# Channel mixers of an encoder trunk: down of 28 of 32 hidden blocks in pairs, seven block products in place of eight

## The chip, the cores and the metric

One core of a Trainium2 chip runs the whole trunk. The metric is the device time of one execution in microseconds (us); the median of the runs counts.

## The reference

Two requests, 256 prompt tokens and 1024 sample tokens of 1024 channels in float32, pass two layers. Layer 0 mixes tokens by a bidirectional recurrent mixer (RWKV-7), layer 1 by neighbourhood attention; each is followed by the same kind of channel mixer, which is all that changes here:

```python
def _sq_relu_mlp(h, w_up, w_down):
    return jnp.square(jax.nn.relu(h @ w_up)) @ w_down
...
D_FF = 4 * D_MODEL
...
        x = x + y
        x = x + _sq_relu_mlp(_rms_norm(x, p['norm_mlp_g'][layer]), p['w_up'][layer], p['w_down'][layer])
```

## The kernel before

Activations lie transposed, channels on the 128 partitions and tokens along the free axis: 256 prompt tokens (segment 0) and two segments of 512 sample tokens (1 and 2). Float32 products are made of three matmuls in the float32r format: each operand is cut into a high part (a cast by ACT) and a low part (the difference, by DVE or POOL), and `mm3` (lines 95 to 97) adds high x high, high x low and low x high into one bank of PSUM. So every weight that is loaded is cut too (`wsplit`, lines 88 to 90: transfer, cast, low part).

`channel_layer` does, for each layer, the output projection of the token mixer, the channel mixer and the first work of what follows. The 4096 hidden channels go in 32 blocks of 128 (`f`). For a block, `up(f, s)` multiplies the up weights with the 8 x 128 input channels of a segment (`dense`, 24 matmuls), takes relu on ACT (line 1360), squares on POOL (1361) and cuts the result into `hh` and `hl` (1363 on ACT, 1364 on DVE). `down` multiplies the block's 128 hidden channels into 8 groups of 128 output channels (3 matmuls each) and DVE adds each group from PSUM to the running sum `x` (1382). The up weights of a block (512 KB) and its down weights (512 KB) are transferred once, on SP's queue, as one tile each.

`x` is kept divided by the norm's factor during the loop (`scale`, line 1347), and the factor is multiplied back at the end of the last `down` (1384). PSUM has eight banks: seven rotate for all products, one serves the norms. The loop from block 2 on runs up of block `f` and down of block `f - 1` for each segment; the last two blocks' downs are added in one bank. Instructions are put in order on each engine by a planner, by the order of the text and by when their operands will be there; only in the last part of each layer PE's order is that of the text:

```python
            for f in range(2, NF - 1):
                for s in range(3):
                    up(f, s)
                    down([f - 1], s)
                if rest and f > 4:
                    inverse(*rest.pop())
                wdown(f)
...
            with tc.manual_schedule(engines={mybir.EngineType.PE}):
```

A tile of a pool is one of `bufs` slots that share a `tag`; a tile that takes a slot waits until the slot's last users are done.

Of the kernel before, what the change touches and what calls it, by code (L numbers as in the profile page):

```python
# [13 lines left out]
P = 128  # L14
# [21 lines left out]

class Pieces:
# [11 lines left out]
class Trunk:  # L49
    def __init__(self, ctx, tc, a):  # L50
# [16 lines left out]
        self.dall = self.cp.tile([P, 8, 2, 20], F32, name="dall")  # L67
        self.bonus = self.cp.tile([P, 20, 8], F32, name="bonus")
# [436 lines left out]
    def v_block(self, act, vw, dst, tp, pp, q, tb, scale=1.0, later=False):  # L505

        nc = self.nc
        ps = pp[0].tile([P, 512], F32, name="vps", tag=pp[1])
# [648 lines left out]
    def add_squares(self, wk, x, m, s, acc, nsq=2):  # L1157
# [6 lines left out]
        else:  # L1164
            sq = wk.tile([P, 512], F32, name="sq", tag="sq", bufs=nsq)
# [11 lines left out]
    def token_norms(self, wk, wh_, pn, acc, s):  # L1177
# [8 lines left out]
        for j in range(2):  # L1186
            for b in range(nb):
                if j and b % 2 == 0:

                    w = 4 // nb  # L1190
                    pq = wh_.tile([P, 256], F32, name="pq", tag="hhFalse", bufs=2)
# [12 lines left out]
    def gate_begin(self):  # L1204
# [36 lines left out]
        def weight(m):  # L1241
            self.wo.append(self.wsplit(self.clw, self.a["w_o"][m], 1024, nc.gpsimd, tag="u"))
# [11 lines left out]
    def gated(self, wk, pm, src):  # L1254

        nc, act = self.nc, self.act
        with self.gctx, self.tc.tile_pool(name="go", bufs=1, reuse_waits="tile", side="right") as gp:
            (sh, sl, ss), (gh, gl, gs) = self.gate
            todo = [(0, k) for k in range(KT)] + [(s, k) for s in (1, 2) for k in range(KT - 1)] + [(1, KT - 1), (2, KT - 1)]
            for s, k in todo:  # L1260
# [5 lines left out]
                ps = pm.tile([P, 512], F32, name="ps", tag="ps")  # L1266
# [7 lines left out]
    def channel_layer(self, layer, x_src, src, wname, dst, gnext=None, gate=False):  # L1274
# [6 lines left out]
        with ExitStack() as ctx:  # L1281
# [7 lines left out]
            pn = ctx.enter_context(tc.tile_pool(name="cln", bufs=1, space=PSUM, reuse_waits="tile"))  # L1289
            wo = self.wo  # L1290
            if gate:
                self.gated(wk, pm, src)
# [13 lines left out]
            def dense(hi, lo, s):  # L1306
                c0, c1 = SEGS[s]
                n = c1 - c0
                ps = pm.tile([P, 512], F32, name="ps", tag="ps")
# [7 lines left out]
            for seg in ((0, 1), (2,)):  # L1317
                for m in range(8):
                    hi, lo = wo.pop(0)
                    if len(wo) < 1 and todo:  # L1320
                        wo.append(self.wsplit(wp, a[wname][todo.pop(0)], 1024, nc.vector, tag="u"))
# [9 lines left out]
                    for s in seg:  # L1331
# [3 lines left out]
                        self.add_squares(wk, x, m, s, ms[s], 2 + layer)  # L1335
# [17 lines left out]
            def up(f, s):  # L1353
                c0, c1 = SEGS[s]
                n = c1 - c0
                if s == 0:
                    wu[f] = self.wsplit(wp, a["w_up"][layer, f], 1024, nc.gpsimd, tag="u")
                ps = dense(*wu[f], s)
                r = wk.tile([P, 512], F32, name="rl", tag="nt", bufs=3 + layer)
                nc.scalar.activation(r[:, :n], ps[:, :n], AF.Relu)  # L1360
                nc.gpsimd.tensor_tensor(out=r[:, :n], in0=r[:, :n], in1=r[:, :n], op=ALU.mult)  # L1361
                hh, hl = (wh_.tile([P, c1 - c0], F32R, name=t, tag=f"{t}{s > 0}", bufs=4 if s else 2) for t in ("hh", "hl"))
# [558 lines left out]
```

## Time and profile before

| What | Value |
|---|---|
| median of 3 runs | 4051.72 us (4046.44 to 4057.34) |
| span of the profiled execution | 4029.3 us |
| median less span | 22.4 us |
| PE busy | 3805.9 us (94%) |
| DVE, ACT, POOL busy | 2244.2, 1580.9, 1338.7 us |
| MLP loop of layer 0 | about 1500 to 2400 us of the span |
| MLP loop of layer 1 | about 3140 to 4029 us of the span |

The profiled execution's own time is not listed beside its span; times are reckoned from the span and set beside the median of the runs. A row of a group gives the line, the engine, the operation, output and inputs, shapes and count, then busy time in us and mean duration in ns, then the engine's idle time before these instructions and what ended it. A row of a timeline gives start, duration, engine, line, operation; in brackets stands the idle time before it and what ended that. A row of windows gives for each engine its busy time in a stretch and, in parentheses, its instructions, then the clock granted to PE.

### The profile page before, as it was taken

What the parts mean: (1) busy time and instruction counts of PE and PEld (TensorE: products, weight loads), DVE (VectorE), ACT (ScalarE), POOL (GpSimd) and SP (SyncE); (2) the same over time, 40 slices, a digit from 0 to 9 for tenths busy, and PEclk for the clock granted to TensorE, in tenths of its full rate; (3) what the DMA queues carried; (4) which work ended last, traced back from release to release, by engine and by line L of the source; (5) the groups of instructions that cost most, each with busy time, mean ns of one, the idle gap of its engine ahead of it and who ended that gap; (6) DMA issues with size and microseconds to landing.
All of it is one profiled execution on the core that took longest, in us unless ns stands there. A gap on an engine that the chain in (4) does not pass through costs nothing.

```text
span 4029.3 us, 90997 instructions
## 1 busy us (share of the span) xinstructions
PE 3805.9 (94%) x36820; PEld 3210.5 (80%) x36820; DVE 2244.2 (56%) x4581; ACT 1580.9 (39%) x3868; POOL 1338.7 (33%) x1252
## 2 busy tenths in 40 slices
PE   8988898888888899999999999999989999999999
PEld 5764578778888788888888889887778888888888
DVE  5778743656564456555555561455554755555555
ACT  6776642555555431111111142565654111111111
POOL 4446542122222433222222250344443422222222
PEclk9987989999999999999999999999999999999999
DMA  4236565766664421101111015354463010110101
GB/s 140 72 104 221 207 222 137 171 171 160 161 153 118 146 79 37 42 32 42 37 37 43 32 71 165 103 124 98 101 199 129 35 42 35 39 42 32 42 32 63
DMA packets 450885, 394.89 MB, mean 98 GB/s; under 512 B 267456, under 2 KB 352832, under 8 KB 450464
## 3 DMA queue, kind: packets, MB, share of 16 engines
q1 hardware_dynamic: 416048, 327.72, 28.7%
q10 hardware_dynamic: 34416, 61.35, 4.1%
q8 instruction: 289, 4.73, 0.5%
q14 instruction: 132, 1.08, 0.1%
HBM read 270.50 MB, written 124.44 MB: 98 GB/s over the span
## 4 chain that ended last, share of the span: by engine, by line
PE 79%; DVE 6%; ACT 5%; DMA 4%; issue 4%; POOL 2%; SPq 1%; ACTq 0%; DVEq 0%; POOLq 0%
PE ps L95 19%; PE ps L96 19%; PE ps L97 19%; PE wu L997 4%; PE vps L512 1%; PE vps L513 1%; PE vps L514 1%; PE aps L997 1%; PE op L1836 1%; PE kps L997 1%; PE lps L997 1%; PE pt L1779 1%; PE ltw L598 1%; PE yps L997 1%; PE yo L997 1%
## 5 line engine op out<-in xcount | busy, mean ns | idle before, releaser
L1382 DVE TENSOR_TENSOR x<-ps,x 128x256 f32<-128x256 f32 x1488 | 814.5, 597 | 643.8 <-PE ps L97 643.7
L95 PE MATMUL ps<-ah,whi 128*128 128x512 f32 (+1 forms) x2304 | 843.2, 366 | 0.0
L96 PE MATMUL ps<-al,whi 128*128 128x512 f32 (+1 forms) x2304 | 825.5, 358 | 0.0
L97 PE MATMUL ps<-ah,wlo 128*128 128x512 f32 (+1 forms) x2304 | 822.6, 357 | 1.5 <-DVE wlo L90 1.3
L90 POOL TENSOR_TENSOR wlo<-raw,whi 128x1024 fp32r<-128x1024 f32 (+1 forms) x178 | 390.2, 2192 | 856.0 <-ACT whi L89 823.8
L95 PE MATMUL ps<-hh,whi 128*128 128x512 f32 (+1 forms) x1536 | 546.5, 356 | 9.8 <-DVE x L1382 9.8
L96 PE MATMUL ps<-hl,whi 128*128 128x512 f32 (+1 forms) x1536 | 545.6, 355 | 0.0
L97 PE MATMUL ps<-hh,wlo 128*128 128x512 f32 (+1 forms) x1536 | 545.1, 355 | 0.0
L95 PEld LDWEIGHTS ps<-ah,whi 128*128 128x128 f32 x2304 | 434.3, 188 | 72.4 <-issue 8.2
L97 PEld LDWEIGHTS ps<-ah,wlo 128*128 128x128 f32 x2304 | 433.4, 188 | 72.6 <-DVE wlo L90 1.7
L96 PEld LDWEIGHTS ps<-al,whi 128*128 128x128 f32 x2304 | 434.4, 189 | 62.3 <-issue 1.0
L89 ACT CAST whi<-raw 128x1024 fp32r<-128x1024 f32 (+1 forms) x206 | 200.4, 973 | 706.3 <-PE ps L96 627.7
L1361 POOL TENSOR_TENSOR rl<-rl 128x512 f32<-128x512 f32 (+1 forms) x192 | 173.8, 905 | 506.1 <-PE ps L97 462.4
L95 PEld LDWEIGHTS ps<-hh,whi 128*128 128x128 f32 x1536 | 290.7, 189 | 54.2 <-DVE x L1382 12.0
L97 PEld LDWEIGHTS ps<-hh,wlo 128*128 128x128 f32 x1536 | 291.0, 189 | 41.6
L96 PEld LDWEIGHTS ps<-hl,whi 128*128 128x128 f32 x1536 | 290.6, 189 | 40.5
L1360 ACT ACTIVATE rl<-ps 128x512 f32<-128x512 f32 (+1 forms) x192 | 100.7, 524 | 555.9 <-PE ps L97 555.9
L1363 ACT CAST hh<-rl 128x512 fp32r<-128x512 f32 (+1 forms) x192 | 105.6, 550 | 324.2 <-POOL rl L1361 324.2
L1364 DVE TENSOR_TENSOR hl<-rl,hh 128x512 fp32r<-128x512 f32 (+1 forms) x192 | 119.8, 624 | 143.1 <-ACT hh L1363 142.5
L1773 POOL TENSOR_TENSOR s<-s,mx 128x384 f32<-128x384 f32 (+1 forms) x150 | 109.7, 744 | 163.2 <-DVE mx L1772 114.2
L872 DVE TENSOR_TENSOR tmp<-mt,q 128x31 f32<-128x31 f32 (+15 forms) x310 | 117.2, 378 | 38.9 <-ACT mt L861 21.0
L1078 POOL TENSOR_TENSOR y<-y,mu 128x512 f32<-128x512 f32 x18 | 19.3, 1074 | 351.2 <-DVE mu L1075 351.2
(304 smaller groups left out, 8265.1 us busy)
## 6 DMA issues: line engine op xcount, KB each, us to landing
raw<-in_w_down_dram SPq DMA_DIRECT2D x64, 512.0 KB
raw<-in_w_up_dram SPq DMA_DIRECT2D x64, 512.0 KB
ar<-ar_d SPq DMA_DIRECT2D x80, 256.0 KB
bk<-bk_d SPq DMA_DIRECT2D x80, 256.0 KB
ar_d<-ar ACTq DMA_DIRECT2D x32, 512.0 KB
bk_d<-bk ACTq DMA_DIRECT2D x32, 512.0 KB
bs<-tab SPq DMA_DIRECT2D x128, 96.0 KB
v_d<-vt ACTq DMA_DIRECT2D x80, 128.0 KB
```

The lines of the kernel that those rows point to most:

```text
L89: nc.scalar.copy(hi[:, cs], raw)
L90: lo_eng.tensor_tensor(out=lo[:, cs], in0=raw, in1=hi[:, cs].bitcast(F32), op=ALU.subtract)
L95: mm(ps, sh, mh, start=first, stop=False)
L96: mm(ps, sh, ml, start=False, stop=False)
L97: mm(ps, sl, mh, start=False, stop=last)
L872: nc.vector.tensor_tensor(out=tv, in0=mt[:, 0:jj, jj:jj + 1].to_broadcast([P, jj, w]), in1=q[:, jj:jj + 1, jj:].to_broadcast([P, jj, w]), ...
L997: self.nc.tensor.matmul(out, w, x, start=start, stop=stop, skip_group_check=free)
L1361: nc.gpsimd.tensor_tensor(out=r[:, :n], in0=r[:, :n], in1=r[:, :n], op=ALU.mult)
L1363: nc.scalar.copy(hh[:, :n], r[:, :n])
L1364: nc.vector.tensor_tensor(out=hl[:, :n], in0=r[:, :n], in1=hh[:, :n].bitcast(F32), op=ALU.subtract)
L1382: nc.vector.tensor_tensor(out=xv, in0=ps[:, :n], in1=xv, op=ALU.add)
L1773: nc.gpsimd.tensor_tensor(out=s[:, :nk], in0=s[:, :nk], in1=mx[:, 2:3].to_broadcast([P, nk]), op=ALU.mult)
```

## The change

For blocks 2 to 29, two blocks are taken as a pair. Their down on the sample tokens is a product of a 2 x 2 matrix of weight blocks (two halves of 512 output channels, two hidden blocks) with a 2 x 2 matrix of hidden activations (two hidden blocks, two segments). `pair_steps` does it by Winograd's form of Strassen's method: seven block products of sums and differences of the blocks (`prep` makes and cuts them, `product` multiplies), three of which begin on cleared banks while the other four go on adding in the banks of the one before, with each state of a bank added by DVE to the output that it belongs to. The prompt's down takes the four weight halves as they are (`prompt`). `block_pair` writes out an order in which the ups of the next pair stand between the products of this one. Down weights come as two halves of 256 KB in a ring of six. PE follows the order of the text from block 2 on. The seven banks are split into two tags, three (`ps`) and four (`pc`). The second raw buffer of up, output and next-layer weights goes; sum-of-squares scratch and relu tiles share one tag of six; two small tiles of the scan (`dall`, `bonus`) move from the constant pool to one that ends with the scan.

```diff
+MANUAL = {mybir.EngineType.PE}
...
-        self.dall = self.cp.tile([P, 8, 2, 20], F32, name="dall")
-        self.bonus = self.cp.tile([P, 20, 8], F32, name="bonus")
...
-            sq = wk.tile([P, 512], F32, name="sq", tag="sq", bufs=nsq)
+            sq = wk.tile([P, 512], F32, name="sq", tag="nt", bufs=6)
...
-            self.wo.append(self.wsplit(self.clw, self.a["w_o"][m], 1024, nc.gpsimd, tag="u"))
+            self.wo.append(self.wsplit(self.clw, self.a["w_o"][m], 1024, nc.gpsimd, tag="u", rb=1))
...
+            turn = [0]
+
+            def bank(name=None):
+                turn[0] += 1
+                name = name or ("ps", "pc")[turn[0] % 2]
+                return pm.tile([P, 512], F32, name="ps", tag=name, bufs={"ps": 3, "pc": 4}[name])
...
-                ps = pm.tile([P, 512], F32, name="ps", tag="ps")
+                ps = bank(name)
...
-            def up(f, s):
+            def wup(f):
+                wu[f] = self.wsplit(wp, a["w_up"][layer, f], 1024, nc.gpsimd, tag="u", rb=1)
+
+            def split(src, s, pool, tags, bufs, eng):
+                n = src.shape[1]
+                hi, lo = (pool.tile([P, n], F32R, name=t, tag=t, bufs=bufs) for t in tags)
+                nc.scalar.copy(hi, src)
+                eng.tensor_tensor(out=lo, in0=src, in1=hi.bitcast(F32), op=ALU.subtract)
+                return hi, lo
+
+            def cut(f, s, last=False):
+                r = hid[f, s]
+                if last:
+                    hid[f, s] = split(r, s, wh_, ("tt", "tt"), 2, nc.vector)
+                else:
+                    hid[f, s] = split(r, s, wh_, (f"hh{s > 0}", f"hl{s > 0}"), 3 if s else 4, nc.vector)
+
+            def up(f, s, name=None, whole=True):
                 c0, c1 = SEGS[s]
                 n = c1 - c0
-                if s == 0:
-                    wu[f] = self.wsplit(wp, a["w_up"][layer, f], 1024, nc.gpsimd, tag="u")
-                ps = dense(*wu[f], s)
-                r = wk.tile([P, 512], F32, name="rl", tag="nt", bufs=3 + layer)
-                nc.scalar.activation(r[:, :n], ps[:, :n], AF.Relu)
-                nc.gpsimd.tensor_tensor(out=r[:, :n], in0=r[:, :n], in1=r[:, :n], op=ALU.mult)
-                hh, hl = (wh_.tile([P, c1 - c0], F32R, name=t, tag=f"{t}{s > 0}", bufs=4 if s else 2) for t in ("hh", "hl"))
-                nc.scalar.copy(hh[:, :n], r[:, :n])
-                nc.vector.tensor_tensor(out=hl[:, :n], in0=r[:, :n], in1=hh[:, :n].bitcast(F32), op=ALU.subtract)
-                hid[f, s] = hh, hl
-
-            def wdown(f):
-                wd[f] = self.wsplit(wd_, a["w_down"][layer, f], 1024, nc.gpsimd, tag="d", rb=1)
+                ps = dense(*wu[f], s, name)
+                r = wk.tile([P, n], F32, name="rl", tag="nt", bufs=6) if s else wh_.tile([P, n], F32, name="rl", tag="np", bufs=2)
+                nc.scalar.activation(r, ps[:, :n], AF.Relu)
+                nc.gpsimd.tensor_tensor(out=r, in0=r, in1=r, op=ALU.mult)
+                hid[f, s] = r
+                if whole or s == 0:
+                    cut(f, s)
+
+            def wraw(f, i):
+                r = raws[f, i] = wd_.tile([P, 512], F32, name="raw", tag="dr", bufs=6)
+                nc.sync.dma_start(r, a["w_down"][layer, f, :, 512 * i:512 * i + 512])
+
+            def wcut(src):
+                return split(src, 0, wd_, ("dh", "dl"), 4, nc.gpsimd)
+
+            def wdown(f, load=True):
+                for i in range(2):
+                    if load:
+                        wraw(f, i)
+                    wd[f, i] = wcut(raws.pop((f, i)))
 
             def down(fs, s, between={}):
                 c0, c1 = SEGS[s]
                 n = c1 - c0
-                parts = [(wd[f], hid.pop((f, s))) for f in fs]
+                parts = [hid.pop((f, s)) for f in fs]
                 last = NF - 1 in fs
                 if last and gnext is not None:
-                    accs[s] = wk.tile([P, 512], F32, name="acc", tag="acc", bufs=2) if s < 2 else wh_.tile([P, 512], F32, name="acc", tag="hhTrue", bufs=4)
+                    accs[s] = wk.tile([P, 512], F32, name="acc", tag="acc", bufs=2) if s < 2 else wd_.tile([P, 512], F32, name="acc", tag="ds", bufs=2)
                 for m in range(8):
-                    ps = pm.tile([P, 512], F32, name="ps", tag="ps")
-                    for i, ((hi, lo), (hh, hl)) in enumerate(parts):
-                        self.mm3(ps[:, :n], hi[:, m * P:(m + 1) * P], lo[:, m * P:(m + 1) * P], hh[:, :n], hl[:, :n], i == 0, i == len(parts) - 1)
+                    ps = bank()
+                    cs = slice(m % 4 * P, m % 4 * P + P)
+                    for i, (f, (hh, hl)) in enumerate(zip(fs, parts)):
+                        hi, lo = wd[f, m // 4]
+                        self.mm3(ps[:, :n], hi[:, cs], lo[:, cs], hh, hl, i == 0, i == len(parts) - 1)
                     xv = x[s][:, m]
                     nc.vector.tensor_tensor(out=xv, in0=ps[:, :n], in1=xv, op=ALU.add)
                     if last:
...
+            def pair_steps(f0, f1):
+
+                W, B, S, ch = {}, {}, {}, {}
+                A = lambda i, j: raws[(f0, f1)[j], i]
+                b = lambda j, t: hid[(f0, f1)[j], t]
+                tt = lambda eng, o, x_, y_, op: eng.tensor_tensor(out=o, in0=x_, in1=y_, op=op)
+                bcut = lambda src: split(src, 1, wh_, ("hhTrue", "hlTrue"), 3, nc.vector)
+                stile = lambda: wd_.tile([P, 512], F32, name="ds", tag="ds", bufs=2)
+                ttile = lambda: wh_.tile([P, 512], F32, name="ts", tag="tt", bufs=2)
+                sub, add = ALU.subtract, ALU.add
+
+                def prep(n):
+                    if n == 0:
+                        W[0], B[0] = wcut(A(0, 1)), bcut(b(1, 1))
+                    elif n == 1:
+                        S["s"] = stile()
+                        tt(nc.gpsimd, S["s"], A(1, 0), A(1, 1), add)
+                        S["t"] = ttile()
+                        tt(nc.vector, S["t"], b(0, 2), b(0, 1), sub)
+                        W[1], B[1] = wcut(S["s"]), bcut(S["t"])
+                    elif n == 2:
+                        tt(nc.gpsimd, S["s"], S["s"], A(0, 0), sub)
+                        s4 = stile()
+                        tt(nc.gpsimd, s4, A(0, 1), S["s"], sub)
+                        W[2], B[2] = wcut(s4), bcut(b(1, 2))
+                    elif n == 3:
+                        W[3], B[3] = wcut(A(0, 0)), bcut(b(0, 1))
+                    elif n == 4:
+                        tt(nc.vector, S["t"], b(1, 2), S["t"], sub)
+                        W[4], B[4] = wcut(S["s"]), bcut(S["t"])
+                    elif n == 5:
+                        s3 = stile()
+                        tt(nc.gpsimd, s3, A(0, 0), A(1, 0), sub)
+                        t3 = ttile()
+                        tt(nc.vector, t3, b(1, 2), b(0, 2), sub)
+                        W[5], B[5] = wcut(s3), bcut(t3)
+                    elif n == 6:
+                        tt(nc.vector, S["t"], b(1, 1), S["t"], sub)
+                        W[6], B[6] = wcut(A(1, 1)), bcut(S["t"])
+                    elif n == 7:
+                        W[7] = wcut(A(1, 0))
+
+                def product(n):
+                    new, seg, row = ((1, 1, 0), (1, 2, 4), (0, 2, 0), (1, 1, 0), (0, 2, 0), (0, 2, 4), (0, 1, 4))[n]
+                    (hi, lo), (hh, hl) = W[n], B[n]
+                    for j in range(4):
+                        if new:
+                            ch[j] = bank("pc")
+                        cs = slice(j * P, j * P + P)
+                        mm = nc.tensor.matmul
+                        mm(ch[j], hi[:, cs], hh, start=bool(new), stop=False, skip_group_check=True)
+                        mm(ch[j], hi[:, cs], hl, start=False, stop=False, skip_group_check=True)
+                        mm(ch[j], lo[:, cs], hh, start=False, stop=True, skip_group_check=True)
+                        xv = x[seg][:, row + j]
+                        nc.vector.tensor_tensor(out=xv, in0=ch[j], in1=xv, op=ALU.add)
+
+                def prompt(n):
+                    i, j = {0: (0, 1), 3: (0, 0), 6: (1, 1), 7: (1, 0)}[n]
+                    (hi, lo), (hh, hl) = W[n], b(j, 0)
+                    for h in range(2):
+                        ps = bank("ps")
+                        for c in range(2):
+                            cs = slice((2 * h + c) * P, (2 * h + c + 1) * P)
+                            self.mm3(ps[:, 256 * c:256 * c + 256], hi[:, cs], lo[:, cs], hh, hl, True, True)
+                        xv = x[0][:, 4 * i + 2 * h:4 * i + 2 * h + 2].rearrange("p m t -> p (m t)")
+                        nc.vector.tensor_tensor(out=xv, in0=ps, in1=xv, op=ALU.add)
+                return prep, product, prompt
+
+            def block_pair(f2, cur, ahead):
+
+                (prep, product, prompt), f3, final = cur, f2 + 1, ahead is None
+                U = lambda f, s: up(f, s, "ps", False)
+                prep(1)
+                product(0)
+                prompt(0)
+                U(f2, 1)
+                wraw(f3, 0)
+                prep(2)
+                product(1)
+                U(f2, 2)
+                wraw(f2, 1)
+                prep(3)
+                product(2)
+                U(f2, 0)
+                if not final:
+                    wup(f2 + 2)
+                prep(4)
+                product(3)
+                prompt(3)
+                U(f3, 1)
+                wraw(f3, 1)
+                prep(5)
+                product(4)
+                if not final:
+                    U(f3, 2)
+                prep(6)
+                product(5)
+                prep(7)
+                U(f3, 0)
+                wraw(f2, 0)
+                if not final:
+                    wup(f3 + 2)
+                product(6)
+                prompt(6)
+                if not final:
+                    ahead[0](0)
+                prompt(7)
+
+            wu, wd, hid, accs, raws = {}, {}, {}, {}, {}
...
+            wup(0)
             up(0, 0)
             scale(0)
             wdown(0)
+            wup(1)
             up(1, 0)
             up(0, 1)
             up(1, 1)
             scale(1)
             up(0, 2)
+            wup(2)
             down([0], 0)
             down([0], 1)
             scale(2)
             up(1, 2)
             down([0], 2)
+            wup(3)
             wdown(1)
-            for f in range(2, NF - 1):
-                for s in range(3):
-                    up(f, s)
-                    down([f - 1], s)
-                if rest and f > 4:
-                    inverse(*rest.pop())
-                wdown(f)
-            up(NF - 1, 0)
-            up(NF - 1, 1)
-            wdown(NF - 1)
-            norms = lambda s: self.token_norms(wk, wh_, pn, accs[s], s)
-            vw = []
-
-            def block(tb):
-                self.v_block(act, vw, self.scr["v1_d"], (wk, "nt", 512, 3), (pm, "ps"), 0, tb, self.tn[:, 0, tb:tb + 1])
-            N = lambda s: lambda: norms(s)
-            V = lambda tb: lambda: block(tb)
-            with tc.manual_schedule(engines={mybir.EngineType.PE}):
+            with tc.manual_schedule(engines=MANUAL):
+                up(2, 1, None, False)
+                wraw(3, 0)
+                down([1], 1)
+                wraw(2, 1)
+                up(2, 2, None, False)
+                wraw(3, 1)
+                down([1], 2)
+                wraw(2, 0)
+                up(2, 0)
+                wup(4)
+                down([1], 0)
+                up(3, 1, None, False)
+                cur = pair_steps(2, 3)
+                up(3, 2, None, False)
+                cur[0](0)
+                up(3, 0)
+                wup(5)
+                for f in range(2, NF - 2, 2):
+                    ahead = pair_steps(f + 2, f + 3) if f < NF - 4 else None
+                    block_pair(f + 2, cur, ahead)
+                    cur = ahead
+                    if rest and f > 4:
+                        inverse(*rest.pop())
+                wdown(NF - 2, False)
+                cut(NF - 2, 1)
+                wdown(NF - 1, False)
+                cut(NF - 1, 1)
+                cut(NF - 2, 2)
+                up(NF - 1, 2, None, False)
+                cut(NF - 1, 2, True)
                 down([NF - 2, NF - 1], 0)
-                up(NF - 1, 2)
...
-                    v0 = [self.wsplit(wp, a["w_nv"][0, :, 4 * j:4 * j + 4, :].rearrange("p k c -> p (k c)"), 1024, nc.gpsimd, tag="u") for j in range(2)]
+                    v0 = [self.wsplit(wp, a["w_nv"][0, :, 4 * j:4 * j + 4, :].rearrange("p k c -> p (k c)"), 1024, nc.gpsimd, tag="u", rb=1) for j in range(2)]
...
-        self.l0_proj()
-        self.scan()
+        with self.tc.tile_pool(name="lead", bufs=1) as lead:
+            self.dall = lead.tile([P, 8, 2, 20], F32, name="dall")
+            self.bonus = lead.tile([P, 20, 8], F32, name="bonus")
+            self.l0_proj()
+            self.scan()
```

More of the change, by code (lines that the diff above doesn't have):

```diff
@@ L507, in v_block @@
         nc = self.nc
-        ps = pp[0].tile([P, 512], F32, name="vps", tag=pp[1])
+        ps = pp[0].tile([P, 512], F32, name="vps", tag=pp[1], bufs=(*pp, None)[2])
         ts_ = slice(tb * P, (tb + 1) * P)
@@ L1155, in act_tiles, with add_squares @@
         return [(pool.tile([P, T], F32R, name=f"ah{k}"), pool.tile([P, T], F32R, name=f"al{k}")) for k in range(KT)]
-    def add_squares(self, wk, x, m, s, acc, nsq=2):
+    def add_squares(self, wk, x, m, s, acc):
         nc = self.nc
@@ L1252, in gate_begin, with gated @@
         at(11.4, weight, 1)
-    def gated(self, wk, pm, src):
+    def gated(self, bank, src):
         nc, act = self.nc, self.act
@@ L1289, in channel_layer @@
             pn = ctx.enter_context(tc.tile_pool(name="cln", bufs=1, space=PSUM, reuse_waits="tile"))
+            turn = [0]
[3 more added lines that the diff above has]
+                return pm.tile([P, 512], F32, name="ps", tag=name, bufs={"ps": 3, "pc": 4}[name])
             wo = self.wo
             if gate:
-                self.gated(wk, pm, src)
+                self.gated(bank, src)
             xp = pool("xp")
@@ L1304, in channel_layer, with dense @@
             nc.gpsimd.memset(ones, 1.0)
-            def dense(hi, lo, s):
+            def dense(hi, lo, s, name=None):
                 c0, c1 = SEGS[s]
                 n = c1 - c0
-                ps = pm.tile([P, 512], F32, name="ps", tag="ps")
+                ps = bank(name)
                 for k in range(KT):
@@ L1334, in channel_layer @@
                         nc.vector.tensor_tensor(out=x[s][:, m], in0=ps[:, :c1 - c0], in1=x[s][:, m], op=ALU.add)
-                        self.add_squares(wk, x, m, s, ms[s], 2 + layer)
+                        self.add_squares(wk, x, m, s, ms[s])
                 for s in seg:
@@ L1372, in down @@
                 n = c1 - c0
[L1373 removed]
+                parts = [hid.pop((f, s)) for f in fs]
                 last = NF - 1 in fs
                 if last and gnext is not None:
[L1376 removed]
+                    accs[s] = wk.tile([P, 512], F32, name="acc", tag="acc", bufs=2) if s < 2 else wd_.tile([P, 512], F32, name="acc", tag="ds", bufs=2)
                 for m in range(8):
[L1378 to L1380 removed]
+                    ps = bank()
+                    cs = slice(m % 4 * P, m % 4 * P + P)
+                    for i, (f, (hh, hl)) in enumerate(zip(fs, parts)):
+                        hi, lo = wd[f, m // 4]
+                        self.mm3(ps[:, :n], hi[:, cs], lo[:, cs], hh, hl, i == 0, i == len(parts) - 1)
                     xv = x[s][:, m]
@@ new lines, in channel_layer, with block @@
+            wu, wd, hid, accs, raws = {}, {}, {}, {}, {}
+            rest = [(s, j) for s, (c0, c1) in enumerate(SEGS) for j in range((c1 - c0) // P)]
+            norms = lambda s: self.token_norms(wk, wh_, pn, accs[s], s)
+            vw = []
+            def block(tb):
+                self.v_block(act, vw, self.scr["v1_d"], (wk, "nt", 512, 6), (pm, ("ps", "pc")[tb % 2], 3 + tb % 2), 0, tb, self.tn[:, 0, tb:tb + 1])
+            N = lambda s: lambda: norms(s)
+            V = lambda tb: lambda: block(tb)
```

6 lines of the change are left out of this document (2 added, 4 removed).

## The prediction

> **What bounds the kernel now.** I read the page's first two lines, then the windows of the two MLP stages, then the rows of PE and ACT in one stretch, then the groups by shape.
>
> ```profile
> span 4029.3 us, 90997 instructions
> PE 3805.9 (94%) x36820; PEld 3210.5 (80%) x36820; DVE 2244.2 (56%) x4581; ACT 1580.9 (39%) x3868; POOL 1338.7 (33%) x1252
> ```
>
> ```profile
> core 0: us, PE busy (x) PEld busy (x) DVE busy (x) ACT busy (x) POOL busy (x), PEclk, DMA share, GB/s
> 1500.00:1560.00 60.00, 55.59 (x270) 45.55 (x269) 49.66 (x70) 10.05 (x16) 29.91 (x21) 1.00 0.08 27
> 1700.00:1900.00 200.00, 200.00 (x1033) 170.57 (x1032) 105.42 (x193) 38.14 (x58) 55.61 (x37) 1.00 0.11 38
> 3120.00:3180.00 60.00, 55.91 (x287) 46.60 (x286) 55.17 (x70) 14.99 (x25) 37.36 (x26) 0.97 0.12 44
> 3230.00:3430.00 200.00, 200.00 (x1048) 170.91 (x1047) 106.49 (x197) 37.69 (x59) 55.26 (x37) 1.00 0.11 39
> ```
>
> In the two 200 us windows of the block loop (one of each layer) PE is busy 200.00 of 200 us at a granted clock of 1.00. DVE has about 53% there, POOL 28%, ACT 19%. So in the loop PE's own instruction stream sets the time, and any matmul taken out of it shortens the span as long as nothing new arrives late. The two 60 us windows hold the start of each layer's MLP: PE idles 4.4 and 4.1 us there.
>
> ```profile
> 1617.53 1.05 ACT L89 CAST whi<-raw 128x1024 fp32r<-128x1024 f32 x1 [8.44 <-PE ps L96]
> 1645.33 1.05 ACT L89 CAST whi<-raw 128x1024 fp32r<-128x1024 f32 x1 [8.44 <-PE ps L96]
> ```
>
> The same weight cast of two successive blocks is 27.80 us apart, so a pair of blocks takes 55.60 us. Note the 8.44 us that ACT stood waiting for PE: the cast of the next up weights cannot start until the last matmul of a block has let go of the slot.
>
> ```profile
> 1598.06 0.28 PE L95 MATMUL ps<-hh,whi 128*128 128x256 f32 x1
> ...
> 1600.93 0.40 PE L95 MATMUL ps<-ah,whi 128*128 128x512 f32 x1
> ...
> 1606.52 0.39 PE L95 MATMUL ps<-hh,whi 128*128 128x512 f32 x1
> ...
> 1611.97 0.39 PE L95 MATMUL ps<-ah,whi 128*128 128x512 f32 x1
> ```
>
> Twenty-four 512-column matmuls of one dense product lie between 1600.93 and 1606.52 (233 ns each), 24 of down between 1606.52 and 1611.97 (227 ns), 24 of 256 columns of down between 1598.06 and 1600.93 (120 ns). The durations in the groups are longer because matmuls overlap; the spacing is what PE pays.
>
> **The change part by part.** *Products.* For blocks 2 to 29 of each layer the sample half of down was, per pair, 2 blocks x 2 segments x 8 channel groups x 3 = 96 matmuls of 512 columns. Seven products of 4 chains x 3 make 84. The prompt's 48 of 256 columns stay (four prompt calls x 4 x 3), and up is unchanged. So 12 matmuls go in each of 14 pairs of 2 layers: 336 x 227 ns = 76.3 us, or 2.72 us a pair (55.60 to 52.88). Each takes its weight load with it. The Trainium skill (TensorE: Matmul & The Clock Gate, section Back-to-back issue gap) gives a spacing of N/2.4 + 2.5 ns, for 512 columns an estimated 216 ns; 336 of those are 72.5 us and would put the time 3.8 us higher; the trace has 227, and that decides.
>
> *What spacing the new matmuls get.* Their operands lie in other tiles. The bounds are the two spacings just shown: at 233 ns the remaining 2352 product matmuls would cost 2352 x 6 ns = 14 us more; at the other end, act moves in memory too (two small tiles leave the constant pool below it), and if all 3072 sample matmuls of up (64 blocks x 48) fell to 227 ns, 18 us would go. I take 0 for both: a product is again three matmuls into one bank from contiguous 512-column tiles, as down is, and up's operands keep their shape.
>
> *The other engines, per pair of 52.88 us.*
>
> ```profile
> L1382 DVE TENSOR_TENSOR x<-ps,x 128x512 f32<-128x512 f32 x992 | 637.3, 686 | 601.2 <-PE ps L97 601.1
> L1382 DVE TENSOR_TENSOR x<-ps,x 128x256 f32<-128x256 f32 x496 | 177.4, 418 | 42.6 <-PE ps L97 42.6
> L90 POOL TENSOR_TENSOR wlo<-raw,whi 128x1024 fp32r<-128x1024 f32 x142 | 343.8, 2421 | 763.7 <-ACT whi L89 763.7
> L1361 POOL TENSOR_TENSOR rl<-rl 128x512 f32<-128x512 f32 x128 | 133.2, 1041 | 504.6 <-PE ps L97 462.4 <-ACT rl L1360 42.1
> L1361 POOL TENSOR_TENSOR rl<-rl 128x256 f32<-128x256 f32 x64 | 40.5, 633 | 1.6
> L1364 DVE TENSOR_TENSOR hl<-rl,hh 128x512 fp32r<-128x512 f32 x128 | 90.8, 709 | 115.2 <-ACT hh L1363 114.8
> L1364 DVE TENSOR_TENSOR hl<-rl,hh 128x256 fp32r<-128x256 f32 x64 | 29.1, 454 | 27.9 <-ACT hh L1363 27.8
> L89 ACT CAST whi<-raw 128x1024 fp32r<-128x1024 f32 x170 | 178.2, 1048 | 637.4 <-PE ps L96 622.5 <-issue 5.9 <-DMA raw<-in_w_down_dram 5.7
> L1363 ACT CAST hh<-rl 128x512 fp32r<-128x512 f32 x128 | 79.6, 622 | 269.3 <-POOL rl L1361 269.3
> L1363 ACT CAST hh<-rl 128x256 fp32r<-128x256 f32 x64 | 26.0, 407 | 54.9 <-POOL rl L1361 54.9
> L1360 ACT ACTIVATE rl<-ps 128x512 f32<-128x512 f32 x128 | 76.1, 595 | 434.5 <-PE ps L97 434.5
> L1360 ACT ACTIVATE rl<-ps 128x256 f32<-128x256 f32 x64 | 24.6, 384 | 121.4 <-PE ps L97 121.4
> ```
>
> DVE now does 32 x 0.686 + 16 x 0.418 + 4 x 0.709 + 2 x 0.454 = 32.4 us. After: 28 product adds and 8 prompt adds (now 512 wide) are 36 x 0.686 = 24.7, seven low halves and four differences 11 x 0.709 = 7.8 (the differences priced by the same-shaped low-half row), two prompt cuts 0.9: 33.4. POOL has 2 x 2.42 + 2 x 2.42 + 4 x 1.04 + 2 x 0.63 = 15.1 now; after, 4.8 for up's low halves, eight half-width low halves at half of 2.42 (9.7), four weight sums at 1.04 (4.2), squares 5.4: 24.1. ACT: 4 x 1.05 + 6.4 = 10.6 now; after, up casts 2.1, eight weight casts and seven activation casts 15 x 0.62 = 9.3, relus 3.1, prompt casts 0.8: 15.3. All stay under 52.88, so the work itself costs nothing. SP issues six transfers a pair for four, of the same bytes; in its queue a half-width raw may wait for one of six slots, with an up raw behind it. The slot comes free with the weight difference of the sixth product, made before the fifth; from there to the up raw's cast PE has two products and two ups, 13.9 us, against 3.14 us to land (row below).
>
> *Latency, which is what the hand-made order must cover.* Operands of product n+1 are prepared from before product n on. The longest chain is the third product's: square 1.04, two sums 2.08, cast 0.62, low half 1.21 = 4.95 us, against a product (12 x 0.227 = 2.72) and an up (5.59), 8.31. The tightest is at the turn of the pair: from the last matmul of the second prompt up, ACT does relu 0.38, the freed up-weight cast 1.05, the prompt cast 0.41, the next pair's first weight cast 0.62; POOL's up low half ends at 1.43 + 2.42 = 3.85 and the first product's low half at 5.06. PE meanwhile has product 2.72 and two prompt calls 2.88 = 5.60. That covers it by 0.5 us, so I charge nothing; without that cover it would be up to 5 us a pair. A chain that continues in its bank must wait for DVE's add of the product before; between two products lies an up of at least 2.88 us, except in the last pair, where one up is moved behind the pair. There four adds (2.74 us) run against 2.72 us of product: between 0 and the 1.78 us of one slow DVE instruction (shown below). I take the middle, 0.9, for each of two layers.
>
> *One raw buffer for two on the up and output weights.*
>
> ```profile
> 1485.52 2.41 POOL L90 TENSOR_TENSOR wlo<-raw,whi 128x1024 fp32r<-128x1024 f32 x1 [3.27 <-ACT whi L89]
> 1487.96 6.15 SPq L88 DMA_DIRECT2D raw<-in_w_up_dram  x2
> 1490.18 1.03 ACT L89 CAST whi<-raw 128x1024 fp32r<-128x1024 f32 x1
> 1491.29 2.46 POOL L90 TENSOR_TENSOR wlo<-raw,whi 128x1024 fp32r<-128x1024 f32 x1 [1.66 <-ACT whi L89]
> ...
> 2461.39 3.14 DMA raw<-in_w_nq_dram
> ```
>
> The second up weight was cast at 1490.18 from data that lay ready; its transfer had begun while the first was still being cut. Now it starts when the first low half ends, 1485.52 + 2.41 = 1487.93; with 3.14 us to land (the last row, the same 512 KB kind), cast 1.03 and POOL 2.46 it is ready at about 1494.6, not 1493.75: 0.9 us later, at a place where PE is right behind it. I take 0.9 in each layer; it is 0 if PE is given other work. In the output projection the same chain (3.14 + cast + low half) still fits in the 8 x 3 x 233 ns = 5.6 us of a weight and its one-weight lead. Inside the loop an up weight has half a pair.
>
> *The start and the tail.*
>
> ```profile
> PE ps L95 <- DVE x L1382: 4.4, 3, 3.2
> ...
> 1511.88 5.10 DVE x L1347 x3
> ```
>
> PE's order is now fixed from block 2 on. Its 4.4 us of idle there (4.1 in the second layer) wait on down's adds, which stand on DVE behind the scaling of x (the chain of waits has 5.10 us of it just before); that scaling stays. Bounds 8.5 us gained or as much lost again; I take 0. The other edits (bank names, shared scratch tags, tiles that move pools) cost PE no instruction: 0, covered by banks that are read a product earlier.
>
> Sum: -76.3 + 1.8 + 1.8 = -72.7 us. The profiled span is 4029.3, 22.4 below the median of 4051.7; so the span should be 3956.6 and the time 4051.7 - 72.7 = 3979.0.
>
> **The rivals.** *A: DVE falls behind at the turn of the pair.* In the run product 6, prompt 6, prompt 7, product 0, prompt 0 PE needs 2.72 + 2.88 + 2.72 + 1.44 = 9.76 us, and the 14 adds of it need 14 x 0.686 = 9.6 of DVE. Prompts and ups share three banks. Any other DVE instruction that lands there delays an add that PE waits on.
>
> ```profile
> 2374.74 0.74 DVE L1175 SCALAR_TENSOR_TENSOR al<-x,vec,ah 128x512 fp32r<-128x512 f32 x1
> 2376.03 1.86 POOL L1167 TENSOR_TENSOR acc<-acc,sq 128x512 f32<-128x512 f32 x1 [1.76 <-ACT sq L1166]
> 2376.66 1.78 DVE L1384 TENSOR_TENSOR x<-x,ms 128x512 f32<-128x512 f32 x1
> ```
>
> A two-operand DVE instruction took 1.78 us beside a POOL instruction that ended at 2377.89, against 0.74 in the clear. Such instructions rise from 6 to 13 a pair, and POOL's share from 15.1/55.6 to 24.1/52.9. One delay of 1.0 us in each pair gives 28 us: 4007. Against it: DVE has 19 us a pair free, and three banks hold about a microsecond of lag. The Trainium skill (SBUF — State Buffer, section Who interferes with whom) says that a DVE instruction with two SBUF inputs and a GpSimd one that reads SBUF exclude each other for the whole instruction; by that rule, these rows agree, the second ending 0.55 us after POOL's.
>
> *B: spacing.* The bounds above: 3961 if up falls to 227 ns, 3993 if the products rise to 233.
>
> *C, the slower side: a weight cast in the wrong place of ACT's queue.* The up-weight cast waits for PE's last matmul of an up (the 8.44 us rows). If the planner queues it ahead of the casts of the product that comes straight after that up (product 3 or 6), PE stands until whi 1.05, then POOL's 2.42 and a low half 1.21 are through, about 4.7 us, less the two matmuls that need no low half: 4.2. That is above the 2.72 gained: with one in every pair 28 x 1.5 = 42 us are lost, about 4094. It decides from 2.6 us of stall a pair on. Against it: in the loop of before a relu stands behind the same waiting cast, and PE never waited; and in the new text the product's casts come before the up's.
>
> **How the numbers follow.** Forecast 0.54, A 0.25, B 0.13, C 0.08. What a measurement can tell from no change is 0.3%, 12 us. Forecast, B and nearly all of A lie below 4039.6: faster 0.88; a heavy A or a mild C within 0.3%: 0.05; slower 0.07. The range goes from B's low end with the 3.6 us of small charges left out (3957, say 3955) to A added to B's upper end (3993 + 28 = 4021); above it lie C and the heavy A. The forecast's own range is 3970 to 3988.
>
> **What would show it.** PE with 36820 - 336 = 36484 matmuls; loop windows still 200.00 of 200, up-weight casts of alternate blocks 52.9 us apart; product matmuls 227 ns apart; DVE near 63% and POOL near 46% in the loop; no PE wait on DVE's adds but in the last pair. Rival A shows as PE waits on the adds of prompt calls, about 14 per layer; B as unbroken PE with another spacing; C as PE waits of 4 us on low halves with an up-weight cast just before. I am wrong if PE's idle time in the loop is above 15 us in sum.

## The result, and the profile after

The changed kernel is slower: 4124.5 us (median of 4 runs) against 4049.1, a ratio of 1.018 (95% interval 1.017 to 1.020), where 3979 was forecast. The page of its profile:

```profile
span 4126.5 us, 90151 instructions
PE 3804.2 (92%) x36484; PEld 3194.2 (77%) x36484; DVE 2414.1 (59%) x4441; ACT 1694.6 (41%) x4128; POOL 1658.0 (40%) x1540
```

The matmuls are 336 fewer, as the change says, and the span is longer. The windows of the block loop (first column the stretch, then each engine's busy time, then the clock granted to PE) answer to the 200.00 of 200 of before:

```profile
core 0: us, PE busy (x) PEld busy (x) DVE busy (x) ACT busy (x) POOL busy (x), PEclk, DMA share, GB/s
1700.00:1900.00 200.00, 192.30 (x969) 162.49 (x968) 124.27 (x172) 50.70 (x88) 92.17 (x70) 0.97 0.12 37
1900.00:2100.00 200.00, 189.75 (x956) 160.27 (x955) 124.08 (x172) 49.64 (x87) 92.27 (x71) 0.97 0.12 38
3250.00:3450.00 200.00, 191.90 (x958) 161.87 (x957) 119.46 (x172) 47.18 (x83) 87.99 (x67) 0.97 0.12 37
```

PE now idles 8 to 10 us in 200, and its clock is 0.97. The list of PE's waits over the whole span names one large new wait, on the adds of the prompt calls (line 1491), 26 times, about once in each pair:

```profile
PE ps L96 <- DVE x L1491: 66.9, 26, 2.6
PE ps L98 <- POOL wlo L91: 5.7, 4, 2.3
```

The turn of a pair is the stretch in which one pair ends and the next begins (product 6, prompts 6 and 7, product 0). One of them shows how the wait comes about, engine by engine; first POOL, then ACT, DVE and PE:

```profile
1723.43 1.62 POOL L1431 TENSOR_TENSOR ds<-ds,raw 128x512 f32<-128x512 f32 x1
1725.13 1.63 POOL L1431 TENSOR_TENSOR ds<-raw,ds 128x512 f32<-128x512 f32 x1
1726.72 2.40 POOL L91 TENSOR_TENSOR wlo<-raw,whi 128x1024 fp32r<-128x1024 f32 x1
1729.09 0.61 POOL L1384 TENSOR_TENSOR rl<-rl 128x256 f32<-128x256 f32 x1
```

```profile
1725.27 0.37 ACT L1383 ACTIVATE rl<-ps 128x256 f32<-128x256 f32 x1
1729.73 0.41 ACT L1367 CAST hhFalse<-rl 128x256 fp32r<-128x256 f32 x1 [4.09 <-POOL rl L1384]
```

```profile
1725.53 1.87 DVE L1480 TENSOR_TENSOR x<-ps,x 128x512 f32<-128x512 f32 x3
1730.16 0.42 DVE L1368 TENSOR_TENSOR hlFalse<-rl,hhFalse 128x256 fp32r<-128x256 f32 x1 [2.76 <-ACT hhFalse L1367]
1730.51 0.68 DVE L1480 TENSOR_TENSOR x<-ps,x 128x512 f32<-128x512 f32 x1
1731.11 2.56 DVE L1491 TENSOR_TENSOR x<-ps,x 128x512 f32<-128x512 f32 x4
```

```profile
1729.00 0.28 PE L98 MATMUL ps<-hhFalse,dl 128*128 128x256 f32 x1
1731.85 0.38 PE L96 MATMUL ps<-hhFalse,dh 128*128 128x256 f32 x1 [2.57 <-DVE x L1491]
```

The relu of the prompt block ends at 1725.64 on ACT. POOL is then in the second of two sums of the next pair's weights (`prep(2)`, 1.62 and 1.63 us; the second began at 1725.13) and has up's low half (2.40) ahead of the 0.61 us square, which runs at 1729.09. ACT's cast of that block waits 4.09 us for it, and DVE's low half 2.76 us for the cast. The fourth add of product 6 and the adds of the prompt calls stand behind that low half in DVE's queue; their inputs had long been there. PE starts its last matmul into the third `ps` bank at 1729.00 and waits until 1731.85. Then it runs at half clock:

```profile
1726.00:1729.00 3.00, 3.00 (x23) 2.81 (x22) 1.41 (x3) 0.00 (x0) 3.00 (x2) 1.00 0.25 81
1732.80:1735.80 3.00, 3.00 (x9) 2.32 (x9) 1.82 (x4) 0.62 (x1) 2.38 (x2) 0.50 0.00 0
```

In that second row 9 matmuls run in 3 us, in the first 23 (mostly of half the width); matmuls of 512 columns start 0.43 us apart in the second and 0.23 apart in product 6, before the wait. A turn thus lost 2.73 us to the wait and, in 20 of 28 turns, about 1.7 to a clock halved for 3.4 us. (In the first turn of each layer the wait is on the cast of the prompt block, 1.8 us; those two are among the 28 and the 20.)

The stages by the traces (us; the first gate product, the first relu of each MLP, the first product of layer 1 behind MLP 0, the first transfer of layer 1's output weights):

| kernel | to gate | gate to up | MLP 0 | to w_no | w_no to up | MLP 1 | end |
|---|---|---|---|---|---|---|---|
| before, as predicted from | 1356.7 | 140.1 | 883.1 | 560.7 | 189.0 | 899.7 | 4029.3 |
| before, once more (e1) | 1370.0 | 141.3 | 884.1 | 559.5 | 189.0 | 899.7 | 4043.6 |
| after | 1381.5 | 141.5 | 916.3 | 574.8 | 194.0 | 918.4 | 4126.5 |
| e4, no pairs | 1372.2 | 142.2 | 899.1 | 561.4 | 196.1 | 903.7 | 4074.6 |
| e5, square on ACT | 1369.5 | 141.8 | 860.7 | 570.5 | 196.1 | 864.4 | 4003.0 |
| e10, best | 1372.3 | 141.5 | 858.8 | 565.4 | 190.1 | 860.2 | 3988.3 |

### The profile page after: what moved, and what is told of

Its sections match the earlier page's. It is cut to its first block, busy times and chain, and to the rows that moved or that the text cites. A ratio compares the mean times of both kernels' runs of the same rounds, so it can differ in the third digit from the quotient of the medians.

```text
span 4126.5 us, 90151 instructions
## 1 busy us (share of the span) xinstructions
PE 3804.2 (92%) x36484; PEld 3194.2 (77%) x36484; DVE 2414.1 (59%) x4441; ACT 1694.6 (41%) x4128; POOL 1658.0 (40%) x1540
## 5 line engine op out<-in xcount | busy, mean ns | idle before, releaser
L1480 DVE TENSOR_TENSOR x<-ps,x 128x512 f32<-128x512 f32 x784 | 528.6, 688 | 434.7 <-PE ps L1478 434.2
L91 POOL TENSOR_TENSOR wlo<-raw,whi 128x1024 fp32r<-128x1024 f32 (+1 forms) x114 | 235.4, 2065 | 224.0 <-ACT whi L90 219.9
L1477 PE MATMUL ps<-hlTrue,dh 128*128 128x512 f32 x784 | 319.5, 408 | 0.0
L1476 PE MATMUL ps<-hhTrue,dh 128*128 128x512 f32 x784 | 318.8, 407 | 0.0
L1478 PE MATMUL ps<-hhTrue,dl 128*128 128x512 f32 x784 | 316.8, 404 | 0.0
L1368 POOL TENSOR_TENSOR dl<-raw,dh 128x512 fp32r<-128x512 f32 x128 | 166.6, 1303 | 148.7 <-ACT dh L1367 107.8
L96 PE MATMUL ps<-hhFalse,dh 128*128 128x256 f32 x512 | 148.4, 290 | 76.8 <-DVE x L1491 66.9
L1478 PEld LDWEIGHTS ps<-hhTrue,dl 128*128 128x128 f32 x784 | 154.7, 197 | 35.3
L1476 PEld LDWEIGHTS ps<-hhTrue,dh 128*128 128x128 f32 x784 | 153.8, 196 | 32.9
L1477 PEld LDWEIGHTS ps<-hlTrue,dh 128*128 128x128 f32 x784 | 154.0, 196 | 30.7
```

The source lines that it names most:

```text
L91: lo_eng.tensor_tensor(out=lo[:, cs], in0=raw, in1=hi[:, cs].bitcast(F32), op=ALU.subtract)
L96: mm(ps, sh, mh, start=first, stop=False)
L1368: eng.tensor_tensor(out=lo, in0=src, in1=hi.bitcast(F32), op=ALU.subtract)
L1476: mm(ch[j], hi[:, cs], hh, start=bool(new), stop=False, skip_group_check=True)
L1477: mm(ch[j], hi[:, cs], hl, start=False, stop=False, skip_group_check=True)
L1478: mm(ch[j], lo[:, cs], hh, start=False, stop=True, skip_group_check=True)
```

## The experiments

**e1: before once more.**

> The kernel before once more, for the spread of its stages from execution to execution. Its profiled span was 4029.3 us, but its runs take 4046 to 4057. If the 25 us by which the changed kernel reaches the channel mixer later, and the 19 us that it takes longer over attention, are only spread, this profile has its first gate product 10 to 25 us later than 1356.7 us too. If they belong to the change, it is within 5 us of 1356.7.

Its gate comes at 1370.0, 13 us later than in the first profile; among the profiles of all kernels here it lies between 1356.7 and 1383.1. The stages behind it repeat within 1.3 us. So at least 13 of the 25 us by which the changed kernel reaches its gate later are spread; that the other 12 are spread too is likely by that range, and not shown. The later columns of the table can be compared, and the 19 us that the changed kernel takes longer over attention (574.8 and 194.0 for 560.7 and 189.0) are its own.

**e2: the prompt's last cut later in the text.**

```diff
+            def up(f, s, name=None, whole=True, late=False):
...
+                if (whole or s == 0) and not late:
...
-                U(f3, 0)
+                up(f3, 0, "ps", False, True)
...
                 prompt(7)
+                cut(f3, 0)
```

> The cut of the prompt's last hidden block of a pair (ACT cast and DVE low half) stands later in the text, behind the second prompt call. Theory H (a blocked queue: DVE's low half of that cut stands ahead of the last add of product 6, waits for POOL and ACT, and PE waits 2.6 us for the banks behind it, after which its clock is halved for 3.4 us; about 3.9 us a pair): PE's waits on the prompt adds fall from 67 us to under 15, halved clock in the loops is gone, 4010 to 4050 us. Rival P (DVE and POOL hold each other up at their port, so DVE is late wherever the cut stands): the wait turns up at another place, 4095 to 4125. Rival R (pools, bank tags and single raw buffers cost the time): above 4080.

4121.5 us, ratio to before 1.019 (1.017 to 1.022): no change against the changed kernel. The time lies in the ranges of P and R, but it decides nothing between them and H, since the edit was no test of H after all: at the turn every queue has the order that it had, and DVE's low half still stands before the fourth add. The planner orders by when it reckons the operands ready, and the later place in the text did not move it.

**e3: the prompt's low halves on POOL.**

```diff
-                    hid[f, s] = split(r, s, wh_, (f"hh{s > 0}", f"hl{s > 0}"), 3 if s else 4, nc.vector)
+                    hid[f, s] = split(r, s, wh_, (f"hh{s > 0}", f"hl{s > 0}"), 3 if s else 4, nc.vector if s else nc.gpsimd)
```

> The prompt's low halves are made by POOL and not by DVE; nothing else. H: DVE has nothing in its queue that waits for POOL at the turn, 4010 to 4060 us. P: POOL gets 28 x 2 instructions more and the port is as busy, 4115 to 4140. R: above 4080.

4129.5 us (ratio 1.022, 1.020 to 1.024), against H as I had put it, and in the ranges of P and R. DVE's rows at a turn, then ACT's:

```profile
1711.83 2.47 DVE L1480 TENSOR_TENSOR x<-ps,x 128x512 f32<-128x512 f32 x4
1716.99 0.80 DVE L1368 TENSOR_TENSOR hlTrue<-rl,hhTrue 128x512 fp32r<-128x512 f32 x1 [2.69 <-ACT hhTrue L1367]
```

```profile
1716.03 0.40 ACT L1367 CAST hhFalse<-rl 128x256 fp32r<-128x256 f32 x1 [4.04 <-POOL rl L1384]
1716.34 0.61 ACT L1367 CAST hhTrue<-rl 128x512 fp32r<-128x512 f32 x1
```

The four adds of product 6 now run in one piece, but the next DVE instruction in line is another low half, whose cast stands on ACT behind the prompt's cast, which still waits for POOL's square. The prompt adds stand behind that one. So the row that was moved is not the cause by itself; what is late in both kernels is the head of the chain, POOL's square. H was mended to that, and e5 and e6 test it.

**e4: all edits but the pairs.** The loop of before, with the new pools, banks, tags, half-width down weights and single raw buffers:

```diff
+            for f in range(2, NF - 1):
+                wup(f) if f > 3 else None
+                for s in range(3):
+                    up(f, s)
+                    down([f - 1], s)
...
+                wdown(f)
```

> All edits but the pairs: eight products for eight in the loop order of before, with the new pools, bank tags, half-width down weights, single raw buffers and shared tags. H: close to before, 4045 to 4070 us (one late up weight and the start: 0 to 20). R: 4080 to 4110, that is most of what is lost outside the loop. P: as H.

4080.1 us (ratio 1.009, 1.007 to 1.011): 35 us lost without any pair, above H's range and just at the lower edge of R's. In its loop nothing is lost:

```profile
1700.00:1900.00 200.00, 200.00 (x1032) 170.16 (x1031) 105.94 (x195) 38.01 (x67) 56.53 (x44) 1.00 0.12 39
3250.00:3450.00 200.00, 200.00 (x1054) 171.50 (x1053) 107.17 (x198) 38.30 (x67) 56.40 (x45) 1.00 0.13 42
```

The loss lies at the starts and ends of the MLPs (15 us in layer 0, 4 in layer 1) and in the second output projection (7).

**e5: the prompt's square on ACT.**

```diff
-                nc.gpsimd.tensor_tensor(out=r, in0=r, in1=r, op=ALU.mult)
+                if s:
+                    nc.gpsimd.tensor_tensor(out=r, in0=r, in1=r, op=ALU.mult)
+                else:
+                    nc.scalar.activation(r, r, AF.Square)
```

> The square of the prompt's hidden block is done by ACT (a second activation) instead of POOL; POOL's queue order is else untouched. Theory H, mended after e2 and e3: what holds PE at the turn is a chain through three in-order queues: POOL does two weight sums (1.63 us each) and up's low half (2.40) before the prompt's 0.61 us square; ACT's casts and DVE's low halves and adds stand behind it. With the square out of POOL that chain is cut at its head: PE's waits on prompt adds under 15 us of 67, no halved clock in the loops, 4010 to 4055 us. Rival P (DVE and POOL at one port, whatever the order): the wait stays above 1 us a pair, 4080 to 4125.

4009.7 us, ratio 0.991 (0.987 to 0.994): 115 us less than the changed kernel (110 when each is set against the times of before in its own session), and below before. PE no longer waits on the adds of the prompt calls anywhere. The loop windows, and POOL, ACT, DVE and PE at a turn:

```profile
1700.00:1900.00 200.00, 200.00 (x1051) 170.83 (x1050) 140.85 (x190) 60.44 (x105) 99.99 (x70) 1.00 0.13 40
2100.00:2300.00 200.00, 200.00 (x1051) 170.82 (x1050) 138.60 (x188) 60.20 (x105) 97.44 (x68) 1.00 0.13 41
```

```profile
1704.32 1.62 POOL L1434 TENSOR_TENSOR ds<-ds,raw 128x512 f32<-128x512 f32 x1
1706.03 1.63 POOL L1434 TENSOR_TENSOR ds<-raw,ds 128x512 f32<-128x512 f32 x1
1707.61 2.69 POOL L91 TENSOR_TENSOR wlo<-raw,whi 128x1024 fp32r<-128x1024 f32 x1
```

```profile
1706.15 0.37 ACT L1383 ACTIVATE rl<-ps 128x256 f32<-128x256 f32 x1
1706.55 0.42 ACT L1387 ACTIVATE rl<-rl 128x256 f32<-128x256 f32 x1
1707.00 0.41 ACT L1367 CAST hhFalse<-rl 128x256 fp32r<-128x256 f32 x1
```

```profile
1704.83 1.67 DVE L1434 TENSOR_TENSOR ts<-rl,ts 128x512 f32<-128x512 f32 x1
1707.62 0.41 DVE L1368 TENSOR_TENSOR hlFalse<-rl,hhFalse 128x256 fp32r<-128x256 f32 x1
```

```profile
1705.11 0.40 PE L1479 MATMUL ps<-hhTrue,dh 128*128 128x512 f32 x1
...
1707.85 0.28 PE L96 MATMUL ps<-hhFalse,dh 128*128 128x256 f32 x1
```

POOL still does the two sums and up's low half in that order, the low half even slower (2.69 for 2.40); ACT goes from relu to square to cast in 1.3 us without it; PE goes from product 6 to the prompt with no gap, and the clock stays at 1.00. The prompt's low half still stands ahead of adds of product 6 in DVE's queue, and delays them by no more than its own 0.41 us, because its cast comes in time. DVE's two-operand difference takes 1.67 us beside POOL here too, so it was not the length of such instructions that held PE.

**e6: POOL's order by hand.**

```diff
-MANUAL = {mybir.EngineType.PE}
+MANUAL = {mybir.EngineType.PE, mybir.EngineType.Pool}
```

> POOL's order in the loop is that of the text too, as PE's is; no instruction changes. In the text the square of the prompt block stands before the up weight's low half and before the next pair's sums. H: same as e5, 4010 to 4055 us; it would also show that the planner's pull-ahead of the sums is the cause, since the work on each engine is the same. P: 4080 to 4125, or more.

4073.8 us (ratio 1.007, 1.004 to 1.009): some 50 better than after, 64 worse than e5; between H and P. PE's waits in layer 0's loop, a window of it, and a turn on ACT, POOL and DVE:

```profile
PE ps L96 <- DVE x L1491: 20.1, 13, 1.5
1900.00:2100.00 200.00, 195.38 (x1005) 165.46 (x1004) 128.42 (x176) 53.77 (x93) 96.27 (x75) 1.00 0.12 38
```

```profile
1717.46 0.37 ACT L1383 ACTIVATE rl<-ps 128x256 f32<-128x256 f32 x1
```

```profile
1717.91 0.62 POOL L1384 TENSOR_TENSOR rl<-rl 128x256 f32<-128x256 f32 x1 [2.28 <-ACT rl L1383]
1718.48 2.40 POOL L91 TENSOR_TENSOR wlo<-raw,whi 128x1024 fp32r<-128x1024 f32 x1
```

```profile
1719.00 2.16 DVE L1368 TENSOR_TENSOR hlFalse<-rl,hhFalse 128x256 fp32r<-128x256 f32 x1 [0.19 <-ACT hhFalse L1367]
```

The square now runs 0.08 us after the relu. But up's low half starts right behind it, and DVE's 0.42 us low half of the prompt, begun at 1719.00, takes 2.16 and ends 0.28 us after POOL's instruction. PE still waits 1.5 us a pair. This is rival P's mechanism, shown here at a place where PE waits behind it. The Trainium skill (SBUF — State Buffer, section Who interferes with whom) has it so: such an instruction with two SBUF inputs waits out the GpSimd one; the trace agrees. None of the waits of 1.5 us, 13 in each layer, was followed by a lower clock.

**e7: e4 with two raw buffers, at the four places that load `u`** (the ends of the lines are shown); the ring of down halves is cut to four to make room.

```diff
-    tag="u", rb=1)
+    tag="u")
-    tag="dr", bufs=6)
+    tag="dr", bufs=4)
```

> e4 (all edits but the pairs) with the second raw buffer of the up, output and next-layer weights given back; the ring of down halves is cut from six to four to make room, two are in use there. If the single raw buffer is what the other edits cost: 4045 to 4060 against 4080 of e4, and PE's waits on up's low half at the start of the MLPs (2.1 and 1.4 us) and the halved clock behind them are gone. If it is the banks, tags or moved tiles: 4070 to 4085.

4061.3 us (ratio 1.004, 1.002 to 1.005), 19 less than e4 and 1 above the range expected for the raw buffer. The wait on up's low half at the start of layer 0's MLP, in e4

```profile
PE ps L98 <- POOL wlo L91: 3.1, 2, 2.1
```

is gone. So in this loop without pairs the single buffer costs about 19 us, and some 17 of the other edits' 35 remain, most of it 11 us in MLP 0 and 5 in the second projection. One wait at the end of MLP 0, which e4 and e7 have and e1 has not, is 4.2 of the 11; which edit causes it was not tested:

```profile
PE vps L513 <- DVE x L1416: 4.2, 1, 4.2
```

**e8: e5 and e6 together.** The edits of both.

> e5 and e6 together. H: within 10 us of the better of the two, since both take away the same wait. P: above 4080.

4050.3 us (ratio 1.001, 1.000 to 1.003): 41 worse than e5, so this missed. With POOL's order fixed, PE waits 0.7 us on 13 prompt adds in each layer, 18 of the 41 us, and longer in the first turn of each layer (2.8 us on a prompt low half, where e5 has 0.9). The order of the text is not the best one for POOL; it only was better than the planner's with the square on it.

**e9 and e10: towards a better kernel.** e9 is e5 with the raw buffer as two halves (`cuts=2` at the four places; the ends of the lines are shown), e10 also puts the last up back where it was:

```diff
-    tag="u", rb=1)
+    tag="u", cuts=2)
...
-                up(NF - 1, 2, None, False)
-                cut(NF - 1, 2, True)
                 down([NF - 2, NF - 1], 0)
+                up(NF - 1, 2, None, False)
+                cut(NF - 1, 2, True)
```

> e5 with the single 4 KB raw buffer of up, output and next-layer weights used as two of half the width: each weight comes, is cast and cut in two halves, in the same memory. e7 got 19 us back from e4 by two whole buffers. If the late weights at the start of each MLP and in the output projection are the cost: 3990 to 4002, against 4010 of e5; the PE waits on up's low half (3.0 and 2.3 us) go. The price is one more cast (2 x 0.62 for 1.05 us) and one more low half (2 x 1.29 for 2.41) on ACT and POOL per weight; if that makes POOL late at the turn of the pair again, 4015 to 4060 with waits on the prompt adds.

> e9 with the last up of a layer (block 31, second sample segment) put back between the prompt's and the first sample segment's down, as in the kernel before. In e5's trace the way from the first up to the first product of the next layer gained 23 us on before in layer 0 and 35 in layer 1; if the new place of that up is what layer 0 lacks, 3 to 10 us better than e9; if it is the start of the MLP or the sums of squares on POOL, the same within 3 us.

e9: 3994.2 us, ratio 0.988 (0.986 to 0.990), 16 better than e5 and in the range expected if late weights were the cost; the waits on up's low half at the start of the MLPs are gone. e10: 3990.1, ratio 0.987 (0.985 to 0.989); its 4 us on e9 are within the intervals, so that step is not decided. The page of e10:

```profile
span 3988.3 us, 90661 instructions
PE 3747.1 (94%) x36484; PEld 3157.6 (79%) x36484; DVE 2443.0 (61%) x4469; ACT 1733.8 (43%) x4288; POOL 1636.8 (41%) x1544
```

## Why the prediction was wrong

The forecast missed by 145.5 us. About 109 of it was lost at the turns of the pairs, which the sum charged with nothing, and 35 is what e4 loses without any pair.

- **Products and their spacing: right.** 36484 matmuls ran. In e5 a product's twelve lie between 1705.11 and 1707.85, 228 ns each. The MLPs take 860.7 and 864.4 us in e5, 899.1 and 903.7 in e4: 38.4 and 39.3 us saved, where half of 336 x 227 ns, the share of one layer, gave 38.1. Rival B's bounds were not needed.
- **Work of each engine: the shares came out, in part by luck.** DVE has 62% and POOL 46% in the changed kernel's loop, where 63 and 46 were reckoned, but a pair there takes 57.2 us on the mean (12 pairs from 1675.85 to 2362.17) and not 52.88. In it DVE has 35.7 us of work for 33.4 and POOL 26.5 for 24.1: the weight sums, priced at 1.04 us, took 1.3 to 1.6, and the 512-column low halves of DVE, priced at 0.71, took 1.1 on the mean. The conclusion held, since neither engine's work fills a pair in e5 either (DVE 70%, POOL 50%).
- **Latency at the turn: the step that failed.** I wrote that 0.5 us of cover remains and charged nothing. The chain behind that went on ACT from the relu to the prompt's cast and left out the prompt's square on POOL, which stands between them. With its 0.63 us in POOL's queue my own 5.06 becomes 5.69, against 5.60 of PE's work: there was no cover even in the order of the text, and in e6, which has that order on POOL, PE does wait 1.5 us a turn, there for a slow low half on DVE. The chain also took POOL's queue to be in the order of the text. The planner runs `prep(2)` two products ahead, and put two POOL sums and up's low half before the square, which began 3.45 us after its relu had ended. And it looked at product 0's operands alone, while PE came to wait for a bank, behind adds that DVE had queued after the late low half. "Without that cover it would be up to 5 us a pair" is above what was lost, 2.73 of waiting at most turns and 1.2 of clock on the mean; that it is near is luck, since it priced another wait and no clock. In all the turns lost about 109 us; between after and e5 the two MLPs differ by 55.6 and 54.0.
- **Rival A named the place and the sign, not the mechanism.** Its waits on the prompt adds came 13 in a layer (14 were said), at 2.6 and not 1.0 us, from a queue on POOL and not from slow DVE instructions. A DVE instruction that a POOL one held up, A's mechanism, made 1.5 us a pair in e6. Rival C's kind of mechanism, an instruction queued ahead of a more urgent one, and its bound (it decides from 2.6 us a pair on; 3.9 were lost) were right; it sat on POOL, not on ACT, and the time lies above C's 4094 too.
- **Single raw buffer: mis-sized.** 1.8 us charged, about 19 measured in the loop without pairs (e4 less e7); two half buffers gave 16 with the pairs (e5 less e9). I priced one late weight at one place; between the traces of e4 and e7, 4 us of it lie in MLP 0 (899.1 against 894.9 in e7), 2.5 in the second projection and up's start behind it (196.1, 193.6) and 7 in MLP 1 (903.7, 896.9).
- **The span against the median.** I took 22.4 us as lying around the span. In after the profiled run took 4128.3 for a span of 4126.5: it is 1.8, and the first profile was a short execution (gate at 1356.7). The forecast itself took 72.7 from the median and does not rest on it.
- **Start and tail.** The start's longest wait on DVE stayed at 3.2 us, so the 0 charged for it held. The tail's step (0.9 a layer) was too low in layer 0: behind MLP 0 the pair kernels take 6 to 15 us more to the next weights (e10 565.4, e5 570.5, after 574.8, against 559.5). Why is open.

## What to carry to other kernels

A latency budget made of durations holds only for the order in which the queues will really run: when one engine's order is written by hand and the others are planned, ask of each short instruction on the critical hand-over what the planner may pull in front of it, and write down every link of the chain, the shortest too. Where a short step joins a chain of three engines, take out the engine that has long, deferrable work (here 0.6 us of squaring off POOL was worth 110 to 115 us). Price a wait on PE with the halved clock behind it, and check text edits against the queues' real order before reading a time as a verdict.

## What the runs showed of the hardware

In the changed kernel 18 of 26 PE waits of 2.57 us, and both waits of 1.8 us in the first turns, were followed by 3.4 us at half clock; of the waits of 1.5 us in e6 none was. What spared the other eight turns is open. The Trainium skill (TensorE: Matmul & The Clock Gate, section HAM oscillation — how this bites in real kernels) asks for no idle gaps above about 3.4 us; here shorter ones sufficed, and the trace decides. In e6 a DVE low half of 256 columns grew from 0.42 to 2.16 us beside a POOL subtraction of 2.40, with PE waiting behind it.
